# Sixteen feed-forward tiles instead of twelve in Strassen's form, with their token operands stored already split

## The chip, the cores and the metric

The kernel runs on one core of a Trainium2 chip. The metric is the device time of one execution in microseconds (us); less is better. The core has five engines that run beside each other: TensorE (PE in the profile) multiplies matrices into the eight banks of PSUM; VectorE (DVE), ScalarE (ACT) and GpSimd (POOL) do the elementwise work; SyncE (SP) issues the transfers between DRAM and SBUF. An engine works off its own instructions in order, and waits on semaphores for the others.

## The reference, cut to what matters

The kernel computes one step of a decoder layer for 1024 prompt tokens and 8 sample tokens (1032 columns in all). The part that the change touches is the SwiGLU feed-forward block:

```python
h2 = rms_norm(x, norm_ffn_pre)
gg, uu = jnp.split(h2 @ w_ffn_in, 2, axis=-1)      # 1024 -> 2 x 2816
f = (jax.nn.silu(gg) * uu) @ w_ffn_out             # 2816 -> 1024
x = x + rms_norm(f, norm_ffn_post)
```

Before it come attention, the convolution branch and their merge, behind it a gated per-layer embedding. The outputs are the new token vectors, the updated key/value caches (mostly shifted copies of the old ones) and the convolution states.

## The kernel before

**Operands in two parts.** The data are 32-bit floats. TensorE takes them in the form float32r, so each operand is held as a high part (rounded by an ACT copy) and a low part (DVE or POOL subtracts the high part from the original). A product is three matmuls (`mm3`, lines 288 to 290): high by high, high by low, low by high. Activations lie with features on the 128 partitions and tokens along the free axis, so the hidden vector of 2816 features is 22 tiles, `NH = 22`, of 128 x 1032.

**The first product** (`w_ffn_in`). Tiles 0 to 2 (`CLASSIC = 3`) are made plainly (`hidden_plain`) and stored to the DRAM scratch `d_h`. Tiles 3 to 21 go through `hidden_strassen(j, nxt)`: a Strassen (Winograd) form with seven products instead of eight, on quarters of 258 tokens (`QN`). Two token halves `p` are worked off side by side; for each product `m` in `ORDER = (1, 2, 6, 5, 7, 3, 4)` and each half there are 12 matmuls of 258 columns, so 168 per tile. `Quad.after(m)` empties PSUM: ACT copies (`p`) after products 1, 6 and 5, DVE additions after 2, 7 and 3, a DVE multiplication after 4. The finished tile lies in a slot called `pk`. Banks come from a ring of seven, six of which a tile uses, so the next tile's second and third bank wait for the emptying after product 4 of this one. Beside the products a generator, `prepare(j + 1)`, makes the weights of the next tile (ACT copies and POOL sums and subtractions, `wah` to `wd`), one step per product.

**From the first to the second product.** `hidden_store(j, p)` writes a tile out at the tile's end. For the tiles that the second product takes in Strassen's form (4 to 15, six pairs) it stores three pieces of the pair and, with the pair's second tile, makes four sums of quarters on DVE (`ts`, four subtractions of 258 columns for each half `p`) and stores them to `d_s`. These are plain 32-bit values; the split in high and low parts is left to the reader of `d_s`.

**The second product** (`w_ffn_out`), in three parts. (1) Tiles 0 to 3 (`PLAIN0 = 4`) plainly: `ffn_out` runs over three token chunks of 344 (`LC`) and eight output tiles, 4 x 3 matmuls of 344 columns each, 24 x 12 = 288, and an ACT copy starts the accumulator `fac`. (2) The six pairs in three groups of two (`PER = 2`): for each group `g` four quarters (token half `p`, output half `half`), each with 7 products x 2 quads (`OutQuad`) of 6 matmuls of 258 columns, so 84 per quarter and 336 per group. After each product DVE adds PSUM to the accumulator (`fa<-fa,g`). (3) The last six tiles (16 to 21) plainly again.

**What is prepared beside part 2.** `mix_weights(g, half)` fetches two weight tiles and makes their sums and splits (ACT and POOL, names `wx`, `wsh`, `wsl`); `mix_hidden(g, p)` loads the pair's pieces from `d_s` into `hr` and splits them: ACT copies (`ux`, `ush`) and DVE subtractions (`ux<-hr,ux`, `usl<-hr,ush`). Each is a generator; the list `ahead` says which of them is advanced, one step after every product, in which quarter, one or two quarters before its result is used. For the first group all this stands beside part 1.

**Slots and queues.** All large tiles (`act`) share 43 slots (`NSLOT`) of 128 x 1032; weights come in through three `raw` slots. In the first product 16 slots hold `h2` and 12 the token sums (`tsum`), and 7 hold the weights of one tile. SP issues all transfers in one order. The 32 copies of caches and states (DRAM to DRAM, `cache_copies`) are issued one at a time between stages: 19 in the first product, the others in parts 1 and 2.

Of the kernel before, what the change touches and what calls it, by code (L numbers as in the profile page):

```python
# [16 lines left out]
P = 128  # L17
# [22 lines left out]
QN = 258  # L40
# [14 lines left out]
PLAIN0, PAIRS, PER = 4, 6, 2  # L55
# [3 lines left out]
def decoder_step(ctx: ExitStack, tc: tile.TileContext, ins, outs):  # L59
# [87 lines left out]
    d_s = scratch("d_s", (PAIRS, 2, P, 7 * QN))  # L147
# [275 lines left out]
    pairs = [(PLAIN0 + 2 * i, PLAIN0 + 2 * i + 1) for i in range(PAIRS)]  # L423
    LAST0 = PLAIN0 + 2 * PAIRS
    wi_ff = {j: w_rows(w_ffn_out, j) for j in range(PLAIN0)}
    wi_fs = {}
# [4 lines left out]
    for j in range(LAST0, NH):  # L431
        wi_ff[j] = w_rows(w_ffn_out, j)
# [1026 lines left out]
    def hidden_store(j, p):  # L1459

        t0 = 2 * p * QN
        pk = packs[j]
        if not PLAIN0 <= j < LAST0:
            SY.dma_start(d_h[j, :, t0:t0 + 2 * QN], pk[:, t0:t0 + 2 * QN])
            return
        i, e = divmod(j - PLAIN0, 2)
        d = d_s[i, p]
        if e == 0:
            SY.dma_start(d[:, 4 * QN:5 * QN], pk[:, t0:t0 + QN])
            return  # L1470
        SY.dma_start(d[:, 5 * QN:], pk[:, t0:t0 + 2 * QN])
        b11, b12, b21, b22 = (y[:, t0 + o:t0 + o + QN] for y in (packs[j - 1], pk) for o in (0, QN))
        ts = act("ts")
        t2, t1, t3, t4 = (ts[:, q * QN:(q + 1) * QN] for q in range(4))
        V.tensor_sub(t1, b12, b11)
        V.tensor_sub(t2, b22, t1)
        V.tensor_sub(t3, b22, b12)
        V.tensor_sub(t4, b21, t2)
        SY.dma_start(d[:, :4 * QN], ts)

    def hidden_strassen(j, nxt):
        pk = packs[j] = act("pk")
        for group in ((0,), (1,)) if j in (CLASSIC, NH - 1) else ((0, 1),):
# [11 lines left out]
            for p in group:  # L1495
                hidden_store(j, p)
# [25 lines left out]
    def first_hidden():  # L1522
        for _ in range(2):
            yield
        yield from plain_hidden(range(PLAIN0))

    prep = prepare(CLASSIC)
    for j in range(CLASSIC, NH):
        for _ in prep:
            pass  # L1530
# [3 lines left out]
    for _ in prep:  # L1534
        pass

    fac = [None] * KT  # L1540

    def ffn_out(js, f, c):
# [96 lines left out]
    def then(*gens):  # L1639
        for x in gens:  # L1640
            yield from x
# [4 lines left out]
    for ci, c in enumerate(LC):  # L1646
        for f in range(KT):
            ffn_out(list(range(PLAIN0)), f, c)
            next(pre, None)
            if f % 4 == 3:  # L1650
                next(copies, None)
# [206 lines left out]
```

## Time and profile before

| what | value |
|---|---|
| three timed runs | 1701.34, 1702.05, 1702.09 us (median 1702.05) |
| the profiled execution | 1698.74 us, its span 1697.0 us |
| PE busy | 1666.4 us (98%) |
| DVE, ACT, POOL busy | 1111.9, 664.5, 378.3 us |
| part 1 of the second product | about 1322.6 to 1372.6 us of the span |
| part 2 (three Strassen groups) | about 1372.6 to 1504.9 us |

A row of the profile names the line, the engine, the operation, `out<-in` by the names of the tiles, and the shapes. Nearly all elementwise work goes through one wrapper and shows as L120, so it is told apart by its tiles. PE matmuls are pipelined: a row shows about 283 ns for one of 258 columns, while a new one starts about every 120 ns, so rates are read from the distance of starts. A wait in brackets is idle time in front of an instruction and names what ended it.

### The profile page before, as it was taken

Reading aid. Unit: us, or ns where it says so; the run is one execution under the profiler, and the core shown is the slowest. Engines: PE = TensorE matmul, PEld = TensorE weight load, DVE = VectorE, ACT = ScalarE, POOL = GpSimd, SP = SyncE. Lnnn points to the kernel's source line nnn. Section 1 sums busy time; section 2 is a strip of 40 time slices with the busy share of each in tenths; the row PEclk is TensorE's granted clock in tenths of the full one; section 3 lists DMA queues with packets and bytes.
Section 4 is the critical chain, followed back from the end, with each engine's and each line's share of the span. In section 5 each row is a group of like instructions: output and inputs, shape, how many; then the busy total and the mean of one; then the engine's idle time right before and its main releaser. Section 6 shows DMA issues by size and latency. Waiting matters only on the chain.

```text
span 1697.0 us, 29372 instructions
## 1 busy us (share of the span) xinstructions
PE 1666.4 (98%) x11795; PEld 1636.1 (96%) x11795; DVE 1111.9 (66%) x1890; ACT 664.5 (39%) x1385; POOL 378.3 (22%) x309
## 2 busy tenths in 40 slices
PE   7999999999999999999999999999999999999998
PEld 7999999999999999999999999999999998999998
DVE  7899879958979676553689344333322258867853
ACT  6434435444342344223445333333332443323520
POOL 1000000000000000000002767666672549400000
PEclk9999999999999999999999999999999999999999
DMA  5241121121354354423332233333333525440411
GB/s 191 65 124 66 44 67 57 50 82 51 102 177 161 101 188 138 128 85 109 96 126 79 94 111 107 107 119 119 125 102 119 197 101 182 147 158 13 154 55 47
DMA packets 89151, 184.21 MB, mean 109 GB/s; under 512 B 11730, under 2 KB 58146, under 8 KB 88630
## 3 DMA queue, kind: packets, MB, share of 16 engines
q1 hardware_dynamic: 88822, 182.21, 32.6%
q8 instruction: 92, 1.51, 0.4%
q0 software_dynamic: 192, 0.13, 0.1%
q14 instruction: 45, 0.37, 0.1%
HBM read 140.92 MB, written 54.88 MB: 115 GB/s over the span
## 4 chain that ended last, share of the span: by engine, by line
PE 87%; DVE 7%; issue 2%; ACT 1%; DMA 1%; POOL 0%; SPq 0%; POOLq 0%; DVEq 0%; ACTq 0%
PE g L288 28%; PE g L289 28%; PE g L290 27%; DVE y L120 3%; DVE ts L120 1%; PE O L691 1%; PE S L646 1%; PE PT L673 1%; DVE pk L120 1%; DVE usl L120 1%; DVE wl L120 1%; DMA raw<-in_w_in_dram 0%; PE m L347 0%; DMA hr<-d_h 0%; PE m L335 0%
## 5 line engine op out<-in xcount | busy, mean ns | idle before, releaser
L288 PE MATMUL g<-hh,wh 128*128 128x384 f32 (+1 forms) x1200 | 393.3, 328 | 7.1 <-ACT wh L120 7.1
L290 PE MATMUL g<-hh,wl 128*128 128x384 f32 (+1 forms) x1200 | 384.5, 321 | 0.2 <-DVE wl L120 0.2
L289 PE MATMUL g<-hl,wh 128*128 128x384 f32 (+1 forms) x1200 | 384.0, 320 | 0.0
L120 DVE SCALAR_TENSOR_TENSOR y<-z,taps,y 128x1023 f32<-128x1023 f32 (+14 forms) x240 | 303.8, 1266 | 36.7 <-ACT y L120 31.1
L288 PEld LDWEIGHTS g<-hh,wh 128*128 128x128 f32 x1200 | 226.5, 189 | 14.4 <-ACT wh L120 7.1
L289 PEld LDWEIGHTS g<-hl,wh 128*128 128x128 f32 x1200 | 226.5, 189 | 0.6 <-DVE hl L120 0.3
L290 PEld LDWEIGHTS g<-hh,wl 128*128 128x128 f32 x1200 | 225.9, 188 | 0.8 <-DVE wl L120 0.8
L120 POOL TENSOR_TENSOR r<-r,mhalf 128x3 f32<-128x3 f32 x18 | 16.4, 908 | 602.3 <-DVE r L120 602.3
L120 DVE TENSOR_TENSOR wl<-raw,wh 128x1024 fp32r<-128x1024 f32 x94 | 114.9, 1226 | 34.6 <-ACT wh L120 28.8
L288 PE MATMUL g<-mh,wh 128*128 128x344 f32 x336 | 108.0, 322 | 0.0
L290 PE MATMUL g<-mh,wl 128*128 128x344 f32 x336 | 107.5, 320 | 0.0
L289 PE MATMUL g<-ml,wh 128*128 128x344 f32 x336 | 107.4, 320 | 0.0
L120 ACT ACTIVATE wh<-raw 128x1024 fp32r<-128x1024 f32 x94 | 98.2, 1052 | 8.8 <-PE g L289 3.8
L120 DVE TENSOR_TENSOR fa<-fa,g 128x258 f32<-128x258 f32 (+1 forms) x192 | 77.5, 430 | 35.6 <-PE g L290 34.0
L120 POOL DMA_DIRECT2D d_st<-st x4 | 2.8, 694 | 412.8 <-ACT E L120 412.7
L120 ACT ACTIVATE p<-g 128x258 f32<-128x258 f32 x114 | 43.4, 383 | 125.0 <-PE g L290 125.0
L288 PE MATMUL g<-mh,wah 128*128 128x258 f32 x304 | 86.5, 284 | 5.4 <-DVE pk L120 5.4
L120 DVE TENSOR_TENSOR pk<-p,g 128x258 f32<-128x258 f32 x76 | 31.9, 421 | 87.9 <-PE g L290 69.8
L120 DVE TENSOR_TENSOR p<-p,g 128x258 f32<-128x258 f32 x38 | 16.1, 424 | 111.7 <-PE g L290 109.1
L120 ACT ACTIVATE sg<-g 128x384 f32<-128x384 f32 (+1 forms) x68 | 30.9, 455 | 145.9 <-PE g L290 123.4
L288 PE MATMUL g<-th,wbh 128*128 128x258 f32 x304 | 86.0, 283 | 0.0
L289 PE MATMUL g<-ml,wah 128*128 128x258 f32 x304 | 86.0, 283 | 0.0
(286 smaller groups left out, 4735.7 us busy)
## 6 DMA issues: line engine op xcount, KB each, us to landing
raw<-in_w_in_dram SPq DMA_DIRECT2D x50, 512.0 KB
raw<-in_w_ffn_in_dram SPq DMA_DIRECT2D x44, 512.0 KB
out_kvs_dram<-in_cache_kv_w_dram SPq DMA_DIRECT2D x16, 510.0 KB
d_s<-ts SPq DMA_DIRECT2D x12, 516.0 KB
hr<-d_s SPq DMA_DIRECT2D x12, 516.0 KB
raw<-in_w_ffn_out_dram SPq DMA_DIRECT2D x24, 256.0 KB
hr<-d_h SPq DMA_DIRECT2D x10, 516.0 KB
raw<-in_w_ffn_out_dram SPq DMA_DIRECT2D x10, 512.0 KB
```

The lines of the kernel that those rows point to most:

```text
L120: ins = fn(*a, **k)
L288: TE.matmul(ps, hi_w, xh, start=first, stop=False, skip_group_check=more)
L289: TE.matmul(ps, hi_w, xl, start=False, stop=False, skip_group_check=more)
L290: TE.matmul(ps, lo_w, xh, start=False, stop=last, skip_group_check=more)
L646: TE.matmul(sp[h][:, o:o + nk], qT[h * 64:(h + 1) * 64, blk * P:(blk + 1) * P], kT[h * 64:(h + 1) * 64, (blk + 1) * P - nk:(blk + 1) * P], ...
L673: TE.transpose(ps[:, o:o + P], e[:, o:o + P], ident)
L691: TE.matmul(ps[h * 64:(h + 1) * 64, i * P:(i + 1) * P], vtok[:, k0:k0 + 64], self.p[half][:, o:o + P], start=kb == kbs[0], stop=kb == kbs[-1])
```

## The change

`PLAIN0` goes and `PAIRS` becomes 8: tiles 3 to 18 are taken in pairs, in four groups of two, and part 1 of the second product falls away. The list `last` holds the six tiles that stay plain, 0, 1, 2, 19, 20 and 21.

```diff
-PLAIN0, PAIRS, PER = 4, 6, 2
+PAIRS, PER = 8, 2
...
-    d_s = scratch("d_s", (PAIRS, 2, P, 7 * QN))
+    d_s = scratch("d_s", (PAIRS, 2, P, 2, 7 * QN))
...
+    pairs = [(CLASSIC + 2 * i, CLASSIC + 2 * i + 1) for i in range(PAIRS)]
+    last = [j for j in range(NH) if all(j not in x for x in pairs)]
```

The pair's sums move out of the tile's end into a generator, `pair_sums`, which is advanced during the next tile, after products 6, 5, 7, 3 and 4 of either half (ten steps). It also makes the split: ACT copies give the high parts (`th`, `bh`), DVE subtractions the low parts, and both go to `d_s`.

```diff
+    def pair_sums(i):
+        a, b = (packs[j] for j in pairs[i])
+        for p in range(2):
...
+            ts, th, bh = act("ts"), act("tsh", F32R), act("bh", F32R)
+            V.tensor_sub(t1, b12, b11)
+            V.tensor_sub(t3, b22, b12)
+            yield
+            V.tensor_sub(t2, b22, t1)
+            V.tensor_sub(t4, b21, t2)
+            A.activation(th, ts, AF.Copy)
+            yield
+            for q in range(2):
+                c = slice(q * 2 * QN, (q + 1) * 2 * QN)
+                V.tensor_sub(ts[:, c].bitcast(F32R), ts[:, c], th[:, c].bitcast(F32))
+            SY.dma_start(d[:, 0, :4 * QN], th.bitcast(F32))
+            SY.dma_start(d[:, 1, :4 * QN], ts)
+            yield
+            A.activation(bh[:, :QN], b11, AF.Copy)
+            A.activation(bh[:, QN:3 * QN], b2, AF.Copy)
+            yield
+            V.tensor_sub(b11.bitcast(F32R), b11, bh[:, :QN].bitcast(F32))
+            V.tensor_sub(b2.bitcast(F32R), b2, bh[:, QN:3 * QN].bitcast(F32))
+            SY.dma_start(d[:, 0, 4 * QN:], bh[:, :3 * QN].bitcast(F32))
+            SY.dma_start(d[:, 1, 4 * QN:5 * QN], b11)
+            SY.dma_start(d[:, 1, 5 * QN:], b2)
+            yield
...
+                    if m not in (1, 2):
+                        next(sums, None)
```

`mix_hidden` loads both parts straight into the slots that the matmuls read; its ACT copies and DVE subtractions are gone.

```diff
-            rb, rt = act("hr"), act("hr")
-            SY.dma_start(rb[:, :3 * QN], d[:, 4 * QN:])
-            SY.dma_start(rt, d[:, :4 * QN])
...
-                split(rb[:, :3 * QN], rest[0][:, :3 * QN], rest[1][:, :3 * QN], V)
...
-            hi, lo = act("ush", F32R), act("usl", F32R)
-            split(rt, hi, lo, V, 2)
+            hi, lo = act("ush"), act("usl")
...
+                for i in range(2):
+                    SY.dma_start(rest[i][:, :3 * QN], d[:, i, 4 * QN:])
...
+            SY.dma_start(hi, d[:, 0, :4 * QN])
+            SY.dma_start(lo, d[:, 1, :4 * QN])
```

The first group's `mix_weights(0, 0)` and `mix_hidden(0, 0)` are now advanced during the first product's last tile, and `mix_weights(0, 1)` in the first quarter, with its sums and subtractions on DVE (new argument `E`) instead of POOL. The accumulators start in the first group: four of its seven products are copied by ACT, three added by DVE. The cache copies are issued two after each tile of the first product and no more later.

```diff
-        prep = prepare(j + 1) if j + 1 < NH else first_hidden()
-        hidden_strassen(j, prep)
-        next(copies, None)
+        prep = prepare(j + 1) if j + 1 < NH else then(mix_weights(0, 0), mix_hidden(0, 0))
+        hidden_strassen(j, prep, sums)
+        for _ in sums:
+            pass
+        if (j - CLASSIC) % 2 and (j - CLASSIC) // 2 < PAIRS:
+            sums = pair_sums((j - CLASSIC) // 2)
+        for _ in range(2):
+            next(copies, None)
...
-            V.tensor_add(c, c, ps)
+            if self.g == 0 and m in (1, 6, 5, 4):
+                A.activation(c, ps, AF.Copy)
+            else:
+                V.tensor_add(c, c, ps)
...
-    pre = then(mix_weights(0, 0), mix_hidden(0, 0), mix_weights(0, 1))
-    for ci, c in enumerate(LC):
-        for f in range(KT):
-            ffn_out(list(range(PLAIN0)), f, c)
-            next(pre, None)
+    pre = iter(())
...
+            if g == 0:
+                ahead[0] = then(mix_weights(0, 1, V), ahead[0])
```

More of the change, by code (lines that the diff above doesn't have):

```diff
@@ L422, in decoder_step @@
         w_cols(w_ffn_in, DFF + j * P)
[L423 to L426, printed above, removed]
+    pairs = [(CLASSIC + 2 * i, CLASSIC + 2 * i + 1) for i in range(PAIRS)]
+    last = [j for j in range(NH) if all(j not in x for x in pairs)]
+    wi_ff, wi_fs = {}, {}
     for g in range(0, PAIRS, PER):
@@ L430, in decoder_step @@
                 wi_fs[i, half] = w_pair(w_ffn_out, pairs[i], half)
-    for j in range(LAST0, NH):
+    for j in last:
         wi_ff[j] = w_rows(w_ffn_out, j)
@@ L1494, in hidden_strassen @@
                     next(nxt, None)
-            for p in group:
-                hidden_store(j, p)
+                    if m not in (1, 2):
+                        next(sums, None)
+            if j in last:
+                for q in quads:
+                    c = slice(q.t0, q.t0 + 2 * QN)
+                    SY.dma_start(d_h[j, :, c], pk[:, c])
         del prods[j]
@@ L1561, in split, with mix_weights @@
             E.tensor_sub(lo[:, a], src[:, a], hi[:, a].bitcast(F32))
-    def mix_weights(g, half):
+    def mix_weights(g, half, E=G):
         H = 2 * P
@@ L1616, in mix_hidden, with then, ffn_out @@
             yield
+    def then(*gens):
+        for x in gens:
+            yield from x
+    prep, sums = prepare(CLASSIC), iter(())
+    for j in range(CLASSIC, NH):
+        for _ in prep:
+            pass
+        prep = prepare(j + 1) if j + 1 < NH else then(mix_weights(0, 0), mix_hidden(0, 0))
+        hidden_strassen(j, prep, sums)
+        for _ in sums:
+            pass
+        if (j - CLASSIC) % 2 and (j - CLASSIC) // 2 < PAIRS:
+            sums = pair_sums((j - CLASSIC) // 2)
+        for _ in range(2):
+            next(copies, None)
+    for _ in prep:
+        pass
+    fac = [None] * KT
+    def ffn_out(js, f, c):
+        t0, n = c
+        ps = gemm_bank_rows([wi_ff[j] for j in js], f, [hid[j] for j in js], c)
+        fv = fac[f][:, t0:t0 + n]
+        V.tensor_add(fv, fv, ps[:, :n])
     class OutQuad:
@@ L1665, in decoder_step @@
                     next(pre, None)
-            next(copies, None)
     for _ in then(pre, plain_hidden(last[5:])):
-        pass
-    for _ in copies:
         pass
@@ L1708, in decoder_step @@
             for k, wi in enumerate(wo):
[L1709 removed]
+                (wh, wl), (xh, xl) = W(wi), hid[last[k]]
                 for f, ps in zip(range(nf, KT), pss):
```

95 lines of the change are left out of this document (27 added, 68 removed).

## The prediction

> **What bounds the kernel now.** I read the page first: which engine is busy, and what the chain that ended last is made of.
>
> ```profile
> span 1697.0 us, 29372 instructions
> PE 1666.4 (98%) x11795; PEld 1636.1 (96%) x11795; DVE 1111.9 (66%) x1890; ACT 664.5 (39%) x1385; POOL 378.3 (22%) x309
> ...
> PE 87%; DVE 7%; issue 2%; ACT 1%; DMA 1%; POOL 0%; SPq 0%; POOLq 0%; DVEq 0%; ACTq 0%
> ```
>
> PE sets the time. An edit helps only if it takes matmuls away or closes a gap between them. So I next took the stretches by time: part 1 (the four plain tiles) and part 2 (the three Strassen groups).
>
> ```profile
> core 0: us, PE busy (x) PEld busy (x) DVE busy (x) ACT busy (x) POOL busy (x), PEclk, DMA share, GB/s
> 1322.60:1372.60 50.00, 46.85 (x290) 46.38 (x289) 10.40 (x12) 20.36 (x39) 22.71 (x24) 0.97 0.45 158
> 1372.60:1504.90 132.30, 125.34 (x1013) 122.39 (x1013) 111.61 (x215) 51.90 (x80) 77.22 (x72) 1.00 0.48 164
> ```
>
> Together 182.3 us. DVE is busy 111.6 of 132.3 us in part 2: nearly a second bound. What must PE take there? A busy PE is not a measure, so I read the pace from the instructions that follow each product: ACT copies in part 1 (one per 12 matmuls of 344), DVE additions in part 2 (one per 6 matmuls of 258), both in stretches without waits, first and last row.
>
> ```profile
> 1361.58 0.46 ACT L120 ACTIVATE fa<-g 128x344 f32<-128x344 f32 x1 [0.92 <-PE g L290]
> 1372.95 0.46 ACT L120 ACTIVATE fa<-g 128x344 f32<-128x344 f32 x1 [1.44 <-PE g L290]
> 1381.06 0.42 DVE L120 TENSOR_TENSOR fa<-fa,g 128x258 f32<-128x258 f32 x1 [0.29 <-PE g L290]
> 1394.01 0.42 DVE L120 TENSOR_TENSOR fa<-fa,g 128x258 f32<-128x258 f32 x1 [0.29 <-PE g L290]
> ```
>
> Six steps in 11.37 us: 1.895 us each, and part 1 has 24: 45.5 us of matmuls in 50.0, so 4.5 us lost. Eighteen steps in 12.95 us: 0.719 us each; a group has 56: 40.3 us, three 120.9 in 132.3, so 11.4 us lost. The waits of PE, before 1330 us (first row) and from there to 1510 (the others), name the causes:
>
> ```profile
> PE g L288 <- DVE pk L120: 5.4, 4, 1.4
> PE g L288 <- DVE fa L120: 4.9, 5, 2.5
> PE g L288 <- ACT uh L120: 3.1, 1, 3.1
> PE g L289 <- DVE ux L120: 1.7, 4, 0.6
> ```
>
> The columns are us in total, times, longest. Part 1 waits once for a load and its split (`uh`); the clock then falls (0.97 over the part). Part 2 waits for DVE: additions late behind splits, and splits late. The rest of the 11.4 is smaller delays of the same sort. In the first product DVE costs 5.4 us at the ends of four pairs. One of them:
>
> ```profile
> 1072.14 2.30 DVE L120 TENSOR_TENSOR ts<-pk,pk 128x258 f32<-128x258 f32 x1
> 1074.69 1.41 DVE L120 TENSOR_TENSOR pk<-pk,p 128x258 f32<-128x258 f32 x1
> 1076.03 1.85 DVE L120 TENSOR_TENSOR ts<-pk,ts 128x258 f32<-128x258 f32 x2
> 1078.14 0.41 DVE L120 TENSOR_TENSOR pk<-g,pk 128x258 f32<-128x258 f32 x1
> 1071.51 2.64 POOL L120 TENSOR_TENSOR wal<-raw,wah 128x1024 fp32r<-128x1024 f32 x1 [6.72 <-ACT pk L120]
> 1074.53 2.73 POOL L120 TENSOR_TENSOR wbl<-s,wbh 128x512 fp32r<-128x512 f32 x2 [0.37 <-PE g L290]
> 1078.60 0.39 PE L288 MATMUL g<-mh,wah 128*128 128x258 f32 x1 [1.34 <-DVE pk L120]
> ```
>
> A subtraction of two SBUF tiles takes 2.30 us where the addition that reads PSUM takes 0.41, and ends as POOL's `wal` ends. The emptying after product 4 (1078.14) comes late, and the next tile's matmul waits 1.34 us for its bank.
>
> **The change part by part.**
>
> *Matmuls.* Part 1 goes (45.5 us) and a fourth group comes (40.3): 5.2 us less. Four groups need 161.2 us.
>
> *Gaps of parts 1 and 2.* At most all 4.5 + 11.4 = 15.9 us go. What leaves and what stays on DVE (x count, then us in total and mean ns):
>
> ```profile
> L120 DVE TENSOR_TENSOR fa<-fa,g 128x258 f32<-128x258 f32 x168 | 65.6, 418 | 19.7 <-PE g L290 18.5
> ...
> L120 DVE TENSOR_TENSOR usl<-hr,ush 128x516 fp32r<-128x516 f32 x24 | 23.3, 1011 | 2.2 <-ACT ush L120 2.2
> ...
> L120 DVE TENSOR_TENSOR ts<-pk,ts 128x258 f32<-128x258 f32 x24 | 20.7, 880 | 0.4
> L120 DVE TENSOR_TENSOR ts<-pk,pk 128x258 f32<-128x258 f32 x12 | 17.5, 1456 | 0.0
> ...
> L120 DVE TENSOR_TENSOR ux<-hr,ux 128x516 fp32r<-128x516 f32 x6 | 7.5, 1252 | 0.1
> ...
> L120 DVE TENSOR_TENSOR ts<-pk 128x258 f32<-128x258 f32 x12 | 6.8, 563 | 27.5 <-POOL s L120 27.5
> L120 DVE TENSOR_TENSOR ux<-hr,ux 128x774 fp32r<-128x774 f32 x6 | 6.4, 1064 | 20.1 <-ACT ux L120 20.1
> L120 DVE TENSOR_TENSOR ux<-hr,ux 128x258 fp32r<-128x258 f32 x6 | 5.7, 957 | 12.1 <-ACT ux L120 12.1
> ```
>
> The splits were 23.3 + 7.5 + 6.4 + 5.7 = 42.9 us, all of two SBUF tiles and so open to POOL's blocking. Without them a group asks DVE for 56 x 0.418 = 23.4 of 40.3 us, and the pace above (no gap from 1381.06 to 1394.01) is what such a stretch looks like. So for groups 1 to 3 I keep 1 us of gaps; bounds 0 and 15 (all gaps as now, four thirds of 11.4).
>
> *The first quarter.* Part 1 gave `mix_weights(0, 1)` 50 us of cover; now it has one quarter, 14 x 0.719 = 10.1 us, and it is needed in steps through the next one, the last low part about 5.8 us in (eight products), so 15.9 us. DVE makes 16 sums and subtractions: ten of 256 columns and six of 512. At the undisturbed lengths (0.41 to 0.42, and 0.68 by the shortest 516-column `usl`) that is 8.3 us, and with six additions 10.8. At the means above (0.94 for `ts`: 45.0 us over 48; 1.01 for `usl`) it is 15.5 + 2.5 = 18. POOL works meanwhile on the next group's weights: 99.9 us for six halves in the two stretches, 16.7 each. So 0 to some 12 us of gaps; I take 3, as 18 passes 15.9 by 2 and additions wait in between. ACT must do its part in the same 10.1 us:
>
> ```profile
> L120 ACT ACTIVATE p<-g 128x258 f32<-128x258 f32 x114 | 43.4, 383 | 125.0 <-PE g L290 125.0
> ...
> L120 ACT ACTIVATE wsh<-sa 128x512 fp32r<-128x512 f32 x12 | 7.5, 624 | 4.2 <-PE g L289 2.4 <-DVE ux L120 1.8
> ```
>
> Eight copies of PSUM (3.1 us) and eight of weights, at most 0.624 each (5.0): it fits.
>
> *The start of the groups.* `mix_hidden(0, 0)` needs seven slots while the last tile still runs; six come free when the first half's product 7 is through, some 12 us before the tile's end, and it brings 4 x 0.925 = 3.7 MB (two tiles' 7 x 258 columns, in two parts, for each of two pairs). What the queue can carry, and what a collision did there:
>
> ```profile
> 1325.00:1330.00 5.00, 4.33 (x28) 4.04 (x26) 1.83 (x2) 0.37 (x1) 2.51 (x4) 1.00 0.93 324
> 1350.00:1355.00 5.00, 5.00 (x34) 5.00 (x33) 0.00 (x0) 1.72 (x4) 4.28 (x6) 1.00 0.94 377
> 1325.34 5.93 DMA hr<-d_h
> ```
>
> At 324 GB/s 3.7 MB take 11.4 us: just in time, and the first product needs only 2.6 MB of it. I take 2 us; bounds 0 and 8 (a load as late as the 5.93 us one, and a slow clock behind it).
>
> *Transfers of a group.* `mix_hidden` moves twice the bytes: 7.4 MB a group, with 2.1 MB of weights 9.5 MB in 40.3 us, 236 GB/s; at 324 they take 29.3 us. Its cover is two quarters (20.2 us) for 3.7 + 1.05 MB (14.7 us). I cost it at nothing; bound under the rivals. The Trainium skill, "DMA: Bandwidth & Descriptors", Specifications, gives about 358 GB/s as one core's share of the DRAM; by it a group's load would take an estimated 26.5 us, and the trace's 377 GB/s in one stretch is above it.
>
> *The sums in the first product.* Per pair DVE had 8 subtractions of 258 (7.5 us at the mean); it gets ten of 258 and six of 516: 9.4 + 6.1 = 15.5 us. ACT gets 2 x 3 copies (some 4.2 us a pair), SP ten stores for six, and one more cache copy a tile.
>
> ```profile
> 1112.00:1196.00 84.00, 81.30 (x676) 80.89 (x675) 32.61 (x57) 29.68 (x64) 56.95 (x40) 1.00 0.37 120
> 1205.89 0.52 SPq L120 DMA_DIRECT2D out_kvs_dram<-in_cache_kv_w_dram  x1
> ```
>
> In four tiles DVE is busy 32.6 of 84 us; 16 more make 49, under PE. ACT goes from 29.7 to 38. DMA: 1.85 MB more of `d_s` and two copies of half a megabyte per pair are about 69 GB/s on 120, share 0.37 to some 0.6; the raw weights behind a copy on SP wait 0.52 us longer to be issued, with a tile (20 us) of lead. Waits that are new: DVE's low parts wait for ACT's `th`, and behind them on DVE stand the additions after 7 and 3 and the multiplication after 4. Each has three products (4.3 us) until PE needs its bank, the last one two (2.9). The sums are spread over ten products and no longer crowd the tile's end, but they are twice as much. Bounds: nothing left of the 5.4 us, or 24 (eight pairs at twice 1.5). I take 0.5 per pair, 4.0 in all, nearest to the two pairs of six that wait for nothing now: 1.4 us gained. Slots tighten too: the two `pk` of the pair and `ts`, `tsh`, `bh` beside 28 + 7 + 7 + 1 make 48 on 43, so some sums start only when the tile's earlier weights are released; the weights of the next tile are made a tile ahead and hide that.
>
> By the Trainium skill, "SBUF — State Buffer", Who interferes with whom, a DVE instruction with two SBUF inputs and a GpSimd one that reads SBUF shut each other out for the whole instruction; the 2.30 us row beside `wal` agrees. Were every one of the 16 to wait for a whole 512-column POOL piece (half of 2.73 us), DVE would need an estimated 30 us a pair for sums instead of 15.5.
>
> *Sum.* 182.3 - (161.2 + 1 + 3 + 2) = 15.1, and 1.4: **16.5 us less**. Against the profiled execution's 1698.74 us that is 1682.2; the timed median lies 3.3 us above that execution, so 1702.05 - 16.5 = **1685.5 us**.
>
> **The rivals.**
>
> *The sums wait as they do now, 1.5 us in each of eight pairs.* For it: `ts` at 1.46 us mean; against: no crowd at the tile's end. 12 instead of 4 us: 1693.5.
>
> *The first two quarters wait for weights.* For it: DVE as full as the quarter, POOL beside it. 12 instead of 3 us: 1694.5.
>
> *Slower: the token loads set the pace.* Place: groups 1 to 3, PE waiting for `ux` or `ush` from the DMA at every second quarter. It decides from the point where the loads run below 236 GB/s; to lose the 16.5 us and 3.4 more, a group must take 6.6 us longer, 9.5 MB in 46.9 us: 203 GB/s. At 190 it would be 50 us a group: 1685.5 + 29 = 1714. Against it: 324 and 377 above; for it: no stretch longer than 10 us has shown such a rate, the average of part 2 being 164.
>
> *Slots and blocking together hold the first product up* by some 2 us more per pair: 16 us, so 1701.5, about no change; from 2.5 it is slower.
>
> *The gaps were not DVE's*, and only the matmuls' 5.2 us come: 1697. The named waits speak against it.
>
> **How the numbers follow.** Forecast (1676 to 1692) 0.62; sums as now 0.13; first quarters 0.10; matmuls only 0.03; first product held up 0.07; loads 0.05. The low end is 1702.05 - 26.5 (5.2 + 15.9 + 5.4, all gaps gone), 1675.5; the high end, 1698, takes in the two middle rivals and leaves out the last two: **1676 to 1698**. A measurement tells 0.2% (3.4 us) from no change, that is 1698.6. Faster 0.88, same 0.05 (most of the held-up first product), slower 0.07 (loads and the rest of it).
>
> **What would show it.** Right: the stretch from the last `wd` matmul to the first `uh` one takes 165 to 169 us; no `usl` or `ux` on DVE in it; `fa<-fa,g` 0.72 us apart in groups 1 to 3; PE's waits for `pk` under 5 us. Wrong: PE waiting for DMA `ux` or `ush` at a group's start (loads), for DVE `wsl` or `wx` in the second quarter (weights), for `pk` twelve times (sums), or for POOL `wal` in the first product (slots).

## The result and the profile after

The changed kernel takes 1716.56 us (median of 4 runs, 1716.08 to 1717.26) against 1702.07 before (1701.34 to 1702.88): ratio 1.0085, interval 1.0068 to 1.0103. It is slower by 14.5 us; the forecast was 16.5 us less. The profiled execution took 1716.17 us. From its page, the head and the chain that ended last, by engine:

```profile
span 1714.1 us, 29702 instructions
PE 1669.7 (97%) x11843; PEld 1640.4 (96%) x11843; DVE 1148.9 (67%) x1960; ACT 670.4 (39%) x1419; POOL 386.2 (23%) x325
...
PE 83%; DVE 7%; POOL 4%; issue 3%; ACT 2%; DMA 1%; SPq 0%; POOLq 0%; DVEq 0%; ACTq 0%
```

PE still sets the time, but POOL has come onto the chain with 4% (0% before). Where it happened is read by cutting the span at the first `wah` matmul, the last `wd` matmul and the last Strassen matmul of the second product. The stretches of before, columns as in the prediction (length, busy time of each engine, granted clock, DMA share, GB/s):

```profile
933.00:1322.60 389.60, 384.24 (x3195) 383.42 (x3194) 137.50 (x246) 138.51 (x299) 247.68 (x176) 1.00 0.33 110
1322.60:1504.90 182.30, 172.19 (x1301) 168.77 (x1300) 122.01 (x227) 72.25 (x119) 99.94 (x96) 0.99 0.47 162
1504.90:1697.00 192.10, 186.27 (x1187) 184.63 (x1185) 120.44 (x238) 60.09 (x114) 5.11 (x6) 1.00 0.23 77
```

And of after, with three finer ones out of the first product:

```profile
933.90:1358.50 424.60, 397.38 (x3194) 395.32 (x3193) 201.03 (x332) 168.35 (x353) 266.36 (x192) 0.96 0.44 157
1358.50:1522.70 164.20, 162.72 (x1350) 161.90 (x1349) 95.62 (x210) 48.57 (x99) 89.17 (x96) 1.00 0.67 238
1522.70:1714.10 191.40, 185.97 (x1186) 184.18 (x1185) 120.08 (x239) 59.89 (x113) 5.10 (x6) 1.00 0.22 75
...
1210.00:1220.00 10.00, 6.98 (x60) 6.77 (x58) 6.07 (x8) 5.70 (x12) 9.30 (x7) 0.97 0.27 95
1220.00:1230.00 10.00, 10.00 (x60) 10.00 (x61) 6.10 (x13) 3.96 (x9) 0.00 (x0) 0.69 0.79 304
1230.00:1240.00 10.00, 10.00 (x86) 10.00 (x85) 2.70 (x7) 3.45 (x7) 9.02 (x7) 1.00 0.35 102
```

Parts 1 and 2 went from 182.3 to 164.2 us: the gain that the change was to bring is there, 18.1 us. The first product went from 389.6 to 424.6 and took 35.0 back. So the question is the first product. What PE waited for there (us in total, times, longest):

```profile
PE g L288 <- DVE pk L120: 21.8, 7, 4.5
PE g L288 <- DVE p L120: 4.3, 2, 2.8
PE g L288 <- ACT p L120: 1.2, 1, 1.2
```

27.3 us of waits against 5.4 before: 21.9 of the 35.0. The clock takes about the rest: 0.69 in the ten microseconds that follow one such wait, 0.96 over the whole stretch. The wait at 1220 us, in order of time (a choice of ACT, POOL, DVE and PE rows, sorted by start):

```profile
1203.64 1.05 ACT L120 ACTIVATE wah<-raw 128x1024 fp32r<-128x1024 f32 x1
1208.45 0.63 ACT L120 ACTIVATE wbh<-s 128x512 fp32r<-128x512 f32 x1 [3.75 <-POOL s L120]
1208.62 1.51 DVE L120 TENSOR_TENSOR ts<-pk,pk 128x258 f32<-128x258 f32 x1
1210.06 1.51 DVE L120 TENSOR_TENSOR ts<-pk,ts 128x258 f32<-128x258 f32 x1
1211.77 0.28 PE L288 MATMUL g<-mh,wah 128*128 128x258 f32 x1
1215.44 0.63 ACT L120 ACTIVATE wch<-s 128x512 fp32r<-128x512 f32 x1 [1.27 <-POOL s L120]
1216.51 0.71 ACT L120 ACTIVATE pk<-pk 128x258 f32<-128x258 f32 x2
1216.94 2.65 DVE L120 TENSOR_TENSOR pk<-pk,p 128x258 f32<-128x258 f32 x2 [3.93 <-ACT pk L120]
1217.86 1.44 POOL L120 TENSOR_TENSOR wd<-raw,wd 128x512 fp32r<-128x512 f32 x1
1219.51 0.75 DVE L120 TENSOR_TENSOR pk<-g,pk 128x258 f32<-128x258 f32 x2
1219.98 0.58 PE L288 MATMUL g<-mh,wah 128*128 128x258 f32 x1 [3.02 <-DVE pk L120]
```

Tile 16 begins on PE at 1211.77. Its first weights are begun on ACT at 1203.64, 8.1 us ahead, and its last, `wd`, end at 1219.3, 7.5 us after the tile's start. In the kernel before the lead from tile 6 on was 28 to 34 us, and `wd` was done 7 to 11.5 us ahead. Its tile 16:

```profile
1166.08 1.05 ACT L120 ACTIVATE wah<-raw 128x1024 fp32r<-128x1024 f32 x1
1188.03 1.28 POOL L120 TENSOR_TENSOR wd<-raw,wd 128x512 fp32r<-128x512 f32 x1
1199.99 0.28 PE L288 MATMUL g<-mh,wah 128*128 128x258 f32 x1
```

So in the kernel after the weights are made just when the tile ends. ACT works in order and waits for POOL's `s` (3.75, then 1.27 us); behind it stands the Silu `pk<-pk` of the finished tile (1216.51), behind that DVE's `pk<-pk,p` (waits 3.93), then the emptying after product 4 (1219.51), and PE waits 3.02 us for its bank. This holds for tiles 10 to 18. The even ones among them, into whose start the sums begun beside the tile before reach (the `ts` rows at 1208.62 and 1210.06 are theirs), last 23.4 to 27.1 us; the odd ones 20.2, as before. That is some 27 us of loss. Tiles 19 to 21 lose some 13 more (21.9, 27.4 and 24.7 us), although their lead is back at 9 to 20 us, so the late weights are not the whole story.

### The profile page after: what moved, and what is told of

The parts are those of the page before. It is cut to its first block, busy times and chain, and to the rows that moved or that the text cites. A ratio compares the mean times of both kernels' runs of the same rounds, so it can differ in the third digit from the quotient of the medians.

```text
span 1714.1 us, 29702 instructions
## 1 busy us (share of the span) xinstructions
PE 1669.7 (97%) x11843; PEld 1640.4 (96%) x11843; DVE 1148.9 (67%) x1960; ACT 670.4 (39%) x1419; POOL 386.2 (23%) x325
## 4 chain that ended last, share of the span: by engine, by line
PE 83%; DVE 7%; POOL 4%; issue 3%; ACT 2%; DMA 1%; SPq 0%; POOLq 0%; DVEq 0%; ACTq 0%
PE g L288 26%; PE g L290 26%; PE g L289 26%; DVE y L120 3%; POOL s L120 2%; DVE pk L120 1%; PE O L690 1%; PE S L645 1%; POOL wbl L120 1%; DVE ts L120 1%; PE PT L672 1%; POOL wal L120 1%; DVE wl L120 0%; DMA raw<-in_w_ffn_in_dram 0%; PE m L347 0%
## 5 line engine op out<-in xcount | busy, mean ns | idle before, releaser
L120 DVE TENSOR_TENSOR fa<-fa,g 128x258 f32<-128x258 f32 (+1 forms) x216 | 91.4, 433 | 83.7 <-PE g L290 72.5
L120 DVE TENSOR_TENSOR wl<-raw,wh 128x1024 fp32r<-128x1024 f32 x90 | 109.6, 1221 | 34.6 <-ACT wh L120 28.9
L288 PE MATMUL g<-mh,wah 128*128 128x258 f32 x304 | 90.1, 299 | 21.8 <-DVE pk L120 21.8
L120 ACT ACTIVATE wh<-raw 128x1024 fp32r<-128x1024 f32 x90 | 94.1, 1052 | 17.4 <-issue 7.7
L289 PE MATMUL g<-ml,wah 128*128 128x258 f32 x304 | 89.7, 296 | 0.0
L290 PE MATMUL g<-mh,wal 128*128 128x258 f32 x304 | 89.6, 296 | 0.0
L290 PE MATMUL g<-th,wbl 128*128 128x258 f32 x304 | 86.7, 285 | 0.0
```

Source lines behind the costliest of these rows:

```text
L120: ins = fn(*a, **k)
L288: TE.matmul(ps, hi_w, xh, start=first, stop=False, skip_group_check=more)
L289: TE.matmul(ps, hi_w, xl, start=False, stop=False, skip_group_check=more)
L290: TE.matmul(ps, lo_w, xh, start=False, stop=last, skip_group_check=more)
```

## The experiments

Each kernel was timed beside the kernel before on the same chip. The stages are cut as above; "before" stands at 933.0, 389.6, 182.3 and 192.1 us.

| run | median us | ratio (interval) | up to the first Strassen tile | first product | parts 1 and 2 | rest |
|---|---|---|---|---|---|---|
| after | 1716.56 | 1.0085 (1.0068 to 1.0103) | 933.9 | 424.6 | 164.2 | 191.4 |
| e1 six slots more | 1724.69 | 1.0132 (1.0117 to 1.0148) | 932.9 | 431.7 | 164.3 | 191.5 |
| e2 no low parts | 1702.55 | 1.0003 (0.9993 to 1.0012) | 934.0 | 408.7 | 164.3 | 191.8 |
| e3 sixteen tiles alone | 1716.08 | 1.0087 (1.0064 to 1.0109) | 933.0 | 399.0 | 186.9 | 192.0 |
| e4 split store alone | 1701.40 | 0.9997 (0.9988 to 1.0007) | 933.2 | 395.3 | 180.2 | 190.8 |
| e5 one copy a tile | 1719.91 | 1.0107 (1.0090 to 1.0124) | 933.1 | 422.6 | 171.0 | 191.9 |
| e6 before, two copies | 1694.06 | 0.9958 (0.9944 to 0.9973) | 932.6 | 390.7 | 177.6 | 191.9 |
| e7 copies last | 1714.18 | 1.0077 (1.0062 to 1.0092) | 934.3 | 388.3 | 164.1 | 225.4 |
| e8 sixteen alone, one copy | 1710.88 | 1.0055 (1.0040 to 1.0070) | 934.5 | 395.7 | 188.3 | 191.3 |
| e9 copies early | 1709.37 | 1.0045 (1.0030 to 1.0060) | 962.6 | 389.4 | 164.6 | 191.6 |
| e10 before, copies early | 1721.37 | 1.0116 (1.0100 to 1.0131) | 960.7 | 389.2 | 177.2 | 192.1 |
| e11 copies on ACT | 1701.79 | 0.9998 (0.9987 to 1.0009) | 934.3 | 409.4 | 164.9 | 191.4 |
| e12 late weights | 1782.50 | 1.0478 (1.0463 to 1.0494) | 961.6 | 462.1 | 164.7 | 191.4 |
| e13 copies mid | 1738.73 | 1.0217 (1.0193 to 1.0241) | 992.1 | 389.4 | 164.9 | 191.2 |
| e14 copies gate | 1690.40 | 0.9928 (0.9912 to 0.9944) | 933.2 | 386.9 | 164.1 | 201.7 |
| e15 copies early, POOL | 1696.56 | 0.9963 (0.9949 to 0.9976) | 950.3 | 388.4 | 165.1 | 191.7 |
| e16 before, copies gate | 1705.20 | 1.0019 (1.0010 to 1.0029) | 934.4 | 389.6 | 173.7 | 204.0 |
| e17 copies gate, later | 1683.14 | 0.9890 (0.9875 to 0.9905) | 934.8 | 389.6 | 164.2 | 193.1 |
| e18 first product by hand | 1803.42 | 1.0593 (1.0575 to 1.0611) | 933.8 | 517.3 | 164.1 | 191.0 |

### Slots, sums, and each part alone (e1 to e4)

e1 frees six slots and leaves the rest of the change:

```diff
-            tsum[p][j] = act("th", F32R), act("tl", F32R)
+            t0 = act("th", F32R)
+            tsum[p][j] = t0, t0
...
-                V.tensor_sub(lo, t[x][:, :QN], hi.bitcast(F32))
```

> The changed kernel, but the low parts of the token sums are not made and TensorE reads the high part in their place: as many matmuls, six of the 43 slots free all through the Strassen tiles of the first product. Slots theory (the sums of a pair take the slots in which the next tile's weights would be made ahead; POOL makes them late and ACT's copies and DVE's additions queue behind): the stretch of the Strassen tiles falls from 424 us to 390-397, PE's waits for pk and p there from 27 us to under 8, the whole to 1680-1690 us. Load theory (the sixteen two-SBUF subtractions per pair and their mutual blocking with POOL): the same DVE work is there, the stretch stays over 415, the whole at 1710-1718.

First product 431.7, 7 us more than after, and the weights late in the same tiles (8.2 us from tile 11 on). So it is not for want of slots that the weights come late.

e2 leaves out the low parts of the sums, so less of DVE's new work:

```diff
-            for q in range(2):
-                c = slice(q * 2 * QN, (q + 1) * 2 * QN)
-                V.tensor_sub(ts[:, c].bitcast(F32R), ts[:, c], th[:, c].bitcast(F32))
...
-            V.tensor_sub(b11.bitcast(F32R), b11, bh[:, :QN].bitcast(F32))
-            V.tensor_sub(b2.bitcast(F32R), b2, bh[:, QN:3 * QN].bitcast(F32))
```

> The changed kernel without the subtractions that make the low parts of the stored sums and pieces (48 us of DVE); the slots, the ACT copies and all stores stay, what is stored as low part is the unsplit value. Load theory: the stretch of the Strassen tiles falls from 424 us to 390-400 and the whole to 1683-1695. Slots theory: sums still hold the same slots, if for less long; the stretch stays over 408, the whole at 1700-1715.

408.7: 15.9 us of the 35.0 go, 19.1 stay, and the lead still falls to 8.2 us from tile 12 on. Where the weights are late, less work on DVE gains nothing: tiles 12, 14, 16 and 18 last 100.6 us together in both runs, with one wait of PE of 2.9 to 3.0 us in each. What goes, goes in tiles 8 and 10 (8.2 us), whose lead hasn't fallen yet in e2 (33.5 and 22.1 us), and in 19 to 21 (7.8 us).

e3 has sixteen tiles in Strassen's form but the sums, stores and late splits as before (two copies a tile); e4 has twelve tiles, and only the split store:

```diff
 # e3
-    def pair_sums(i):
+    def hidden_store(j, p):
...
+        SY.dma_start(d[:, :4 * QN], ts)
...
+                split(rb[:, :3 * QN], rest[0][:, :3 * QN], rest[1][:, :3 * QN], V)
 # e4
-PAIRS, PER = 8, 2
+PLAIN0, PAIRS, PER = 4, 6, 2
...
+        if (j - PLAIN0) % 2 and 0 <= (j - PLAIN0) // 2 < PAIRS:
+            sums = pair_sums((j - PLAIN0) // 2)
+        next(copies, None)
```

> Sixteen tiles in pairs as in the changed kernel, but sums and stores at the tile's end, unsplit, and the split in the second product, as before. Slots theory and load theory alike: the stretch of the Strassen tiles is 390-394 us, parts 1 and 2 (one stretch of four groups) 176-183 us with DVE's splits in it, the whole 1694-1703. If the larger number of pairs itself or the missing part 1 does the harm: over 400 us in the Strassen tiles, the whole over 1708.

> Twelve tiles in six pairs and part 1 as before, but the sums in the next tile, split and stored in two parts, and loaded without a split. Slots theory and load theory alike: six pairs cost 6/8 of 35 us, the stretch of the Strassen tiles is 410-420 us, part 2 124-128 instead of 132, the whole 1712-1722. If it needs eight pairs to do harm: the stretch 390-400, the whole 1692-1702.

e3 takes 399.0 (390 to 394 was expected by both theories) and e4 395.3, 9.4 and 5.7 more than before. Together with the rest of the change it is 35.0, more than the sum: two parts of the change work on each other. In e3 the lead also falls to 8.2 us in tiles 11 to 17, yet six of these seven tiles last 20.2 us: late weights hurt little while the sums stand, as before, in one block at the tile's end. e3's parts 1 and 2 take 186.9, so without the split in the first product four groups are no gain at all.

### The copies (e5 to e8)

Besides the number of pairs, what mainly sets after's first product apart from e4's is two copies a tile in place of one. e5 is the change with one copy a tile, the rest after each quarter of the second product; e6 is the kernel before with two; e7 is the change with no copy in the first product (two after each bank of part 3); e8 is e3 with one copy.

```diff
 # e5 (e8 the same, from e3)
-        for _ in range(2):
-            next(copies, None)
+        next(copies, None)
 # e6, from the kernel before
-        next(copies, None)
+        for _ in range(2):
+            next(copies, None)
 # e7
-        for _ in range(2):
-            next(copies, None)
...
             accs[ci].add(f, fac[f][:, c[0]:c[0] + c[1]])
             tick(2.9)
+            for _ in range(2):
+                next(copies, None)
```

> The changed kernel with the cache copies issued as before: one after each tile of the first product, the others one after each quarter of the second. Copy theory (two copies per tile stand on SP ahead of the raw weights, the weights of the next tile are then placed 8 instead of 17 to 34 us ahead of their use on ACT, and the sums meet a late POOL and a blocked ACT): the late tiles 10 to 18 vanish, weights 15 us or more ahead, the stretch of the Strassen tiles 395-405 us, parts 1 and 2 164-168, the whole 1685-1697. Load theory (the sums alone): the stretch stays over 415 and the whole over 1705.

> The kernel before with two cache copies after each tile of the first product instead of one, and nothing else. Copy theory: the weights of tiles 11 to 18 are placed 8 us ahead instead of 30-34; without the split sums on DVE that costs what it cost beside unsplit sums, some 5-10 us in the Strassen tiles (395-400), parts 1 and 2 unchanged or 1 us shorter, the whole 1703-1712. Load theory: no change, 1700-1704, weights as far ahead as before.

> The changed kernel with all cache copies moved behind the Strassen groups, two after each output tile of the last six plain tiles' first two chunks. Copy theory: weights 17 to 34 us ahead in all tiles, the stretch of the Strassen tiles 393-402, parts 1 and 2 162-166, the whole 1682-1694, 15 to 30 us under the changed kernel. Load theory: the stretch over 412, the whole over 1702.

> Sixteen tiles with unsplit sums at the tile's end (the third run) and the cache copies issued one at a time as before. Copy theory: weights 30 us ahead as before, the stretch of the Strassen tiles falls from 399 to 390-393 us; parts 1 and 2 stay at 183-190 (the split on DVE is in them, with no part 1 to cover the first weights), the whole 1700-1710. If the third run's loss in the first product came of the eight pairs: it stays at 397-401.

e7 settles the place: without copies the first product takes 388.3 us, 1.3 less than before (1.4 was forecast), and PE waits there 3 us in all. So neither the eight pairs' sums nor the slots cost by themselves; the copies are worth 36.3 us (424.6 to 388.3). e6 shows that it takes the change's sums too: with the same two copies the kernel before loses 1.1 us (395 to 400 was expected), although its lead falls to 8.2 us in tiles 11 to 17.

e5 is the miss that matters. As forecast, its weights are ahead again, 15 to 31 us in tiles 7 to 18 and 12 to 14 in 19 to 21, but its first product takes 422.6 us where 395 to 405 was expected. So a lead of 8 us is not needed for a loss of this size. The first eight copies are of 254 KB, the next sixteen of 510 KB: its tiles 7 to 14 last 20.1 to 21.5 us, 15 to 18 last 21.9 to 26.3. Its longest wait of PE, at the start of tile 20:

```profile
1293.83 0.63 ACT L120 ACTIVATE wch<-s 128x512 fp32r<-128x512 f32 x1 [2.00 <-POOL s L120]
1295.45 3.09 DVE L120 TENSOR_TENSOR ts<-ts,tsh 128x516 fp32r<-128x516 f32 x2 [5.46 <-ACT tsh L120]
1306.17 0.58 PE L288 MATMUL g<-mh,wah 128*128 128x258 f32 x1 [9.69 <-DVE pk L120]
```

ACT's copy `tsh` for the sums stands behind `wch`, DVE waits 5.46 us for it, and the sums that follow on DVE without a break stand ahead of the emptying for which PE waits. e8 has the weights 28 to 34 us ahead in tiles 6 to 21 and takes 395.7, 3.3 less than e3, with 6.1 over the kernel before left.

e6 is even faster than the kernel before, as the copies are gone from parts 1 and 2 (177.6 for 182.3). e7 pays at the end instead (225.4 for 191.4); there PE waits:

```profile
PE m L335 <- DVE acc L120: 13.7, 1, 13.7
PE g L288 <- ACT wh L120: 11.5, 1, 11.5
```

### What the copies do: order or transfer (e9 to e12, e18)

e9 puts all copies into the attention and convolution stage (e10 the same in the kernel before). e11 leaves them where the change has them, but ACT's queue issues them. e12 is e9 with the weights made late: their steps are taken only from a tile's fourth product on, and ACT's part of them keeps the written order. e18 is the change with every instruction but the matmuls of these tiles kept in the written order.

```diff
 # e9 (e10: the same, from the kernel before)
                 triple_bank(i, j, c)
+                if i and c != 1:
+                    next(copies, None)
 # e11
-                    SY.dma_start(kvs[g][b, :Lg - 1].rearrange("s t h d -> s (t h d)"),
+                    A.dma_start(kvs[g][b, :Lg - 1].rearrange("s t h d -> s (t h d)"),
 # e12, from e9
-            A.activation(hi, src, AF.Copy)
+            tc.keep_in_program_order(A.activation(hi, src, AF.Copy))
...
-                    next(nxt, None)
+                    if m in (5, 7, 3, 4):
+                        next(nxt, None)
 # e18
     prep, sums = prepare(CLASSIC), iter(())
+    pinned[0] = True
...
+    pinned[0] = False
```

> All 32 cache copies move out of the first product into the attention and convolution stage, two per three banks, where the DMA share in the changed kernel was 0.14 to 0.36; the rest is the changed kernel. Theory A (the loss of the first product lies in where the copies stand, the rest of the change is as forecast): first product 388 to 392 us as with the copies put last, parts 1 and 2 164, tail 191 to 192, start unchanged, so about 1681 us in all (1678 to 1688), ratio 0.988. Rival B (the transfers themselves cost, wherever they are beside work): the start grows by some of what was lost later, 10 us or more, and the total is 1692 or above. Rival C (the sums cost the first product time even without copies): first product 395 or more.

> The kernel before with the same move of its 32 copies: the control that tells what the change is worth when the copies are out of its way. Theory A: first product 389 to 391 us, parts 1 and 2 about 177.6 as in the run with two copies a tile, tail 192, so 1692 to 1696 us; the change (with the copies early in both) is then worth 11 to 14 us, about the forecast gain of parts 1 and 2 without the copies' part. Rival: parts 1 and 2 of the kernel before come down to 170 or less once no copy runs beside them, and the change is worth 5 us or less.

> The changed kernel with the same copies in the same places, two a tile, issued from ScalarE's queue in place of SyncE's: the same bytes move in the first product, but a weight load or a store of the sums on SyncE's queue no longer stands behind a copy, and the order that the build gives ScalarE has the weights 5 to 6 product copies ahead in every tile, as without copies (in the changed kernel none from the seventh tile on). Theory A (place in the queues and the late weights): first product 388 to 395 us, total 1681 to 1689. Rival B (load of the transfers, sums and copies sharing the DMA engines): first product 410 or more, total 1702 or above.

> The early copies of the first run of this set, and the weights of the next tile made late on purpose: their steps are only taken from the fourth product of a tile on, and ScalarE's part is held to that place, so that in the build's order the weights are one product copy ahead in every tile (5 to 9 otherwise); no copy runs in the first product. Theory A (late weights beside the sums stall the tiles, without any copy): first product 405 to 430 us, tiles of 22 us or more, waits of PE on DVE pk and on the weights, total 1698 or above. Rival B (it needs the copies' transfers): first product 388 to 393 us, total about 1681.

> The changed kernel, copies in their places two a tile, but every instruction of the first product's Strassen tiles but the matmuls is kept in the order in which it is written, on each engine and queue, which the copies cannot move: the weights are five product copies ahead in each tile. Theory A (the order that the copies brought about is the larger part): first product 388 to 400 us, total 1681 to 1693. Rival B (the transfers of copies and sums together are, by keeping the stores of the sums in flight): first product 405 us or more, and ScalarE and GpSimd wait for DMA d_s by 20 us or more in all. The written order may cost something by itself, which would show as waits for other engines and not for d_s.

In e9 the first product is 389.4, as expected, but the stage with the copies takes 28.7 us more (theory A missed the total by 28). e10 loses as much there (27.7 against the kernel before). The largest single wait of PE in that stage of e9 is not for a load:

```profile
429.75 0.66 PE L288 MATMUL g<-hh,wh 128*128 128x384 f32 x1 [8.77 <-DVE z L120]
```

e12 shows that late weights beside the spread sums do it without a copy: 462.1 us. Its waits of PE in the first product:

```profile
PE g L288 <- DVE pk L120: 51.0, 8, 6.7
PE g L288 <- DVE p L120: 7.9, 1, 7.9
```

These are the waits of after, only longer and from tile 6 on. Its weights are no later than after's (a lead of 9.5 us, `wd` done 6 to 8 us after the tile's start), yet its even tiles lose 7 to 10 us where after's lose 3 to 7. So the lead alone doesn't set the price, and with ACT's weights held to the written order e12's 72.7 us over e9 are no measure of after's 35.0.

e11 falls between both theories: 409.4. The weights keep their lead (15 to 33 us) and 15.2 us come back, but 19.8 stay. A wait in e11, with the ACT, POOL and PE rows around it:

```profile
1171.49 0.52 ACTq L120 DMA_DIRECT2D out_kvs_dram<-in_cache_kv_w_dram  x1
1172.94 0.52 ACTq L120 DMA_DIRECT2D out_kvs_dram<-in_cache_kv_w_dram  x1
1181.31 2.49 POOL L120 TENSOR_TENSOR wbl<-s,wbh 128x512 fp32r<-128x512 f32 x2 [4.28 <-DMA d_s<-tsh]
1182.38 0.63 ACT L120 ACTIVATE wch<-s 128x512 fp32r<-128x512 f32 x1 [6.04 <-DMA d_s<-ts]
1183.53 0.36 ACT L120 ACTIVATE p<-g 128x258 f32<-128x258 f32 x1
1183.95 0.53 PE L288 MATMUL g<-th,wch 128*128 128x258 f32 x1 [2.85 <-ACT p L120]
```

Here the weights are early enough, so early that they want slots which the sums still occupy: `wch` takes over the slot of a `ts` whose store to `d_s` is under way, waits 6.04 us for it, and the copy of a finished product (`p`, 1183.53) stands behind it on ACT. All waits of ACT, POOL and DVE for `d_s` in this stretch add up to 41 us in e11, to 26 in e5, to 16 in e14 (the same change without copies there) and to 2 in after, where the late weights no longer need the slots so soon. The sum is no price by itself: it is 19 in the kernel before and 27 in e17 below, whose first products both take 389.6 us. But the stores are slower beside the copies: those that ended such waits had been issued 5.8 us earlier in e11, 5.0 in e5 and 3.5 in e14 (medians of 25, 15 and 20).

So the runs point to two ways in which the copies act. Placed two a tile on SP's queue, they bring an order in which the weights come late; there, in tile 16 at least, it is not the transfers that PE waits for: after issues its last 510 KB copy at 1195.7 us and no other copy before 1229, and tile 16, which begins at 1211.77, still loses 6 us. Where the weights keep their lead, as in e11, the copies slow the stores that hold the slots; this way is read from single waits like the one above, and no run prices it. e5 stands between the two: its stores are slower too, but the wait that was followed back there is one of ACT, POOL and DVE for each other.

e18 was to divide the 35 us between the two and did not. In the written order the stretch takes 517.3 us, with PE waiting mostly for ACT, and ACT waits for the stores of the sums by only 5.1 us in all:

```profile
PE g L288 <- ACT p L120: 69.5, 39, 4.6
```

### What the change is worth, and a version that beats both (e13 to e17)

The copies were then put at other places of the changed kernel: between the banks of the convolution's output and the mixing product (e13), after the banks of the last gate stage (e14, and e16 for the kernel before), in the attention stage but on POOL's queue (e15).

```diff
 # e13
         split_to(gb[:, :n], mixs[f][0], mixs[f][1], c)
+        if f % 2:
+            next(copies, None)
...
         accs[q].add(f, m_c(f, q))
         tick(3.4)
+        next(copies, None)
 # e14 (e16: the same, from the kernel before)
         late.append((f, ci, g))
+        for _ in range(2):
+            next(copies, None)
 # e15, from e9
-                    SY.dma_start(kvs[g][b, :Lg - 1].rearrange("s t h d -> s (t h d)"),
+                    G.dma_start(kvs[g][b, :Lg - 1].rearrange("s t h d -> s (t h d)"),
 # e17, from e14
-        for _ in range(2):
+        for _ in range(2 if pTs else 0):
```

> The changed kernel with the 32 copies spread over the banks of the convolution's output and the mixing product (some 660 to 860 us, DMA share 0.24 to 0.47 in the changed kernel, PE without waits there). Theory A (the copies cost only where something late stands behind them; the change itself is worth what was forecast): the stage up to the first Strassen tile grows by under 6 us, first product 388 to 390, parts 1 and 2 164, total 1680 to 1690. Rival B (copies cost about 28 us wherever they stand beside loads that the work waits for): the stage before grows by 15 us or more, total 1697 or above.

> The changed kernel with the copies in the last stage, two after each gate bank (from about 1590 us of its span on, DMA share 0.10 to 0.46). Theory A: first product 388, parts 1 and 2 164, tail 192 to 205 us, total 1680 to 1695. Rival B (the last loads and the stores of the output stand behind the copies): tail 215 us or more, total 1704 or above.

> The early copies (attention and convolution stage), but issued from GpSimd's queue, which is 2 per cent busy there, so that no load on SyncE's queue stands behind one. Theory A (order and place in the queue made the early copies cost 28 us): the stage up to the first Strassen tile is 933 to 942 us, total 1680 to 1690. Rival B (the transfers cost): the stage stays at 955 or more, total 1702 or above.

> The kernel before with its copies in the last gate stage: the control of the run with the same place in the changed kernel. Theory A: first product 389, parts 1 and 2 177, tail as in that run, so 11 to 16 us slower than that run. Rival: the difference is 5 us or less, and the change brings nothing of its own.

> The run with the copies in the last gate stage, but none before the last operand of the output (pin, which gives pTh and pTl) has been issued: the wait of 4.5 us on pTl should go. Theory A (the tail's extra 10 us come from that load behind six copies): tail 192 to 196 us, total 1680 to 1686. Rival B (they come from the copies' transfers beside the last stores, or from their end): tail 200 us or more, total 1689 or above.

e13 is a miss: the stage ahead of the first product takes 58 us more. PE's longest waits there are for DVE `acc` (10.4 and 8.4 us), while no engine waits for a load by more than 2.2 us at a time. That speaks for a changed order of the engines' work and against held-up data; it was not tested apart. e15 issued sixteen of the copies at 36 to 62 us, and the load of `strow` beside them came late, PE waiting 12.0 us for it (0.9 in after): the stage takes 16.4 us more, where A expected at most 8. e14 loses 10.3 us in the rest and gains 37.7 in the first product: 1690.40 us. The stretches of e14:

```profile
933.20:1320.10 386.90, 383.70 (x3193) 383.28 (x3192) 187.48 (x332) 169.33 (x353) 264.65 (x192) 1.00 0.41 143
1320.10:1484.20 164.10, 162.60 (x1350) 161.89 (x1349) 95.70 (x210) 48.68 (x99) 89.15 (x96) 1.00 0.67 239
1484.20:1685.90 201.70, 188.78 (x1186) 186.06 (x1184) 120.22 (x239) 59.42 (x113) 6.02 (x6) 0.98 0.37 127
```

Its first product is nearly as busy on DVE, ACT and POOL as after's (187.5, 169.3, 264.7 for 201.0, 168.4, 266.4), and the clock is 1.00. The same tile as above, in e14:

```profile
1164.62 1.05 ACT L120 ACTIVATE wah<-raw 128x1024 fp32r<-128x1024 f32 x1
1187.36 1.30 POOL L120 TENSOR_TENSOR wd<-raw,wd 128x512 fp32r<-128x512 f32 x1
1195.19 0.28 PE L288 MATMUL g<-mh,wah 128*128 128x258 f32 x1
```

30.6 us of lead in place of 8.1, and `wd` done 6.5 us ahead. The same stretches of e16, the kernel before with its copies at the same place:

```profile
934.40:1324.00 389.60, 384.23 (x3193) 383.33 (x3193) 136.84 (x249) 142.06 (x304) 251.96 (x180) 1.00 0.28 95
1324.00:1497.70 173.70, 168.80 (x1302) 167.50 (x1302) 112.07 (x223) 68.22 (x115) 91.21 (x92) 1.00 0.41 140
1497.70:1701.70 204.00, 190.16 (x1186) 187.17 (x1184) 120.66 (x238) 59.42 (x113) 6.01 (x6) 0.97 0.36 126
```

With the copies at one and the same place the change is worth 1705.20 - 1690.40 = 14.8 us, with the early copies 1721.37 - 1709.37 = 12.0. In parts 1 and 2 the kernel before gains 8.6 us by the copies' leaving alone (182.3 to 173.7; 4.7 and 5.1 in e6 and e10), so of the 18.1 us there some 9.6 to 13.4 are the change's own.

In e14 PE's longest wait in the rest is 4.5 us for `pTl`, whose load stands behind the first six copies. e17 starts the copies behind it: the rest falls from 201.7 to 193.1, and the whole takes 1683.14 us, 1.1% less than the kernel before, under e6 too. The kernel before with its copies at that late place was not run, so how much of this is the change's own is open.

## Why the prediction was wrong

**Matmuls, gaps, first quarter, start and transfers** were forecast at 167.2 us for parts 1 and 2 and took 164.2. PE waits there 1.5 us in all, for DVE and ACT `fa`; none of the waits that would have shown a step wrong appears there. The transfers ran at 238 GB/s over the whole stretch with no wait of PE for one: the rival of slow token loads is out. One cause in this step was wrong: I put all the gaps of parts 1 and 2 down to DVE and the first load, while 5 to 9 us of them went with the cache copies, which e6, e10 and e16 show.

**The sums in the first product** is the step that failed: forecast 1.4 us less (4.0 us of waits in place of 5.4), at worst 18.6 more (24 in place of 5.4), measured 35.0 more. Its sizes for DVE were not the fault. The rows of after for the sums:

```profile
L120 DVE TENSOR_TENSOR ts<-pk,ts 128x258 f32<-128x258 f32 x32 | 28.0, 874 | 0.3
L120 DVE TENSOR_TENSOR ts<-ts,tsh 128x516 fp32r<-128x516 f32 x32 | 26.8, 877 | 13.9 <-ACT tsh L120 13.9
L120 DVE TENSOR_TENSOR ts<-pk,pk 128x258 f32<-128x258 f32 x16 | 16.5, 1031 | 0.0
L120 DVE TENSOR_TENSOR pk<-pk,bh 128x516 fp32r<-128x516 f32 x16 | 12.1, 755 | 0.0
L120 DVE TENSOR_TENSOR ts<-pk 128x258 f32<-128x258 f32 x16 | 10.2, 638 | 0.2 <-PE g L290 0.2
L120 DVE TENSOR_TENSOR pk<-pk,bh 128x258 fp32r<-128x258 f32 x16 | 8.9, 555 | 0.0
```

102.5 us over eight pairs, 12.8 each, where I had 15.5. The estimate of 30 by the Trainium skill ("SBUF — State Buffer", Who interferes with whom) did not come: it supposed that each of the 16 waits for a whole piece of POOL's, but of these 128 subtractions only 28 took over 1.3 us. What failed is the copy that was put at nothing: a weight load that waits 0.52 us behind a copy, "with a tile (20 us) of lead", and beside it "the weights of the next tile are made a tile ahead and hide that". I took the lead as given. With two copies a tile it fell to 8 us, where the same change without copies there (e14) has 17 to 32, and then ACT's and POOL's work on the weights stood in front of the Silu and the emptying at the tile's end, just where the sums had been spread to. The copies cost 36.3 us (e7 against after). e12 shows that late weights beside the spread sums suffice, e5 that with one copy a tile much the same loss comes with the weights 12 to 31 us ahead.

Without copies there the first product takes what was forecast (388.3 in e7, 389.4 in e9, 386.9 in e14, for 388.2), but the close match is luck: no pair waits at all at its end, where 4.0 us were forecast, and the last tile takes 23 to 26 us instead of 20, since in it DVE makes sums for the first group's weights (`sa`, `sb`) ahead of an addition, and PE waits 2.8 us. That loss had been looked for in parts 1 and 2 (3 us for the first quarter, 2 for the start), which is why they came out under the forecast.

**The rivals.** The one that was nearest, "slots and blocking together hold the first product up", had the place right and the cause wrong: e1 rules the slots out for after, and it priced 2 us a pair above the forecast where 4.6 came (36.4 over eight pairs). The sign to watch, PE waiting for `pk` twelve times, came as seven times, but 3 us long instead of 1.5, with a slow clock behind. My range ended at 1698 since no rival joined the copies with the sums; each alone costs little (e6 1.1 us, e4 5.7).

**What stays open.** How the 35 us divide between order and transfers: e11 gives 15 and 20, but its order differs from after's in other ways too, and e18 did not settle it. Nor is it shown in full what slows after's tiles 19 to 21 and e5's tiles 15 to 21, whose leads are 9 to 20 us; of these only the wait at 1306 us in e5 was followed back. How a copy comes to move the weights in the order that the build makes was seen only by its outcome, not traced to a rule.

## What to carry to other kernels

A step that is "made a tile ahead" has a lead that can be read, from its row to the tile that uses it; read it, and ask what each transfer that is added to the same queue does to it. Transfers that nobody waits for still set when others are placed and land: move them alone first (here that was worth 7 us to the kernel before in e6, and cost it 20 in e10), so that a change isn't charged or credited with their move. Two edits that each cost little may share the same slack; the run with both is the one to price.

## What the runs showed of the hardware

A wait of PE of some 3 us can cost as much again in clock. After the 3.02 us wait at 1219.98 the matmul took 0.58 us in place of 0.28, and the granted clock was 0.69 over the next ten microseconds. The Trainium skill, "TensorE: Matmul & The Clock Gate", Part 1, gives the gate one idle window of about 3.4 us; here shorter waits did it, though not each: in e11 one of 2.54 us was followed by 0.83 over ten microseconds. The same wait for the same addition in the last tile, 2.82 to 2.83 us long, was followed by 1.00 in e14, 0.83 in e7 and 0.70 in e9. So the length of a wait of this size doesn't tell its price, and differences of up to 3 us between first products (386.9 in e14, 389.6 in e17, which has the same code there) are no effect of an edit.

The transfers of after's parts 1 and 2 ran at 238 GB/s for 164 us, at a DMA share of 0.67, and PE waited for none of them. The forecast had rested this step on stretches of 5 us (324 and 377 GB/s).
